# Value weights 48 instead of 32 columns into their tile, and dummy products in FFN block 0 in place of a shifted copy

## The chip, the cores and the metric

The kernel runs on one core of a Trainium2 chip. The core's engines work side by side: TensorE (PE in the profile) multiplies, VectorE (DVE), ScalarE (ACT) and GpSimd (POOL) do the elementwise work, and SyncE (SP) issues transfers. The metric is the device time of one execution in microseconds (us), as the median of several runs. Columns below are columns of 4 bytes in a tile of 128 partitions.

## The reference

The kernel computes two layers over 512 tokens of width 1024 in fp32. Each layer has a mixer and an FFN, each between norms that are modulated by a conditioning vector. Layer 0 mixes with a gated recurrence (HGRN2), layer 1 with dilated attention in three groups of windows. Cut to its core:

```python
for layer in range(DEPTH):                       # 2
    mod = (cond @ ada_w[layer] + ada_b[layer])[:, None, :]
    sh1, sc1, g1, sh2, sc2, g2 = jnp.split(mod, 6, axis=-1)
    u = rms_norm(h, norm_g[layer, 0]) * (1.0 + sc1) + sh1
    y = hgrn2_mixer(...) if layer % 2 == 0 else dilated_attention_mixer(...)
    h = h + (1.0 + g1) * rms_norm(y, norm_g[layer, 1])
    u = rms_norm(h, norm_g[layer, 2]) * (1.0 + sc2) + sh2
    y = swiglu_ffn(u, ffn_w_in[layer], ffn_w_out[layer])
    h = h + (1.0 + g2) * rms_norm(y, norm_g[layer, 3])

def swiglu_ffn(u, w_in, w_out):
    gate, up = jnp.split(u @ w_in, 2, axis=-1)
    return (jax.nn.silu(gate) * up) @ w_out

# dilated_attention_mixer, its first step (3 groups, 8 heads of 128)
proj = (u @ w_in).astype(jnp.float32).reshape(B, S, N_GROUPS, 3, ATT_HEADS, ATT_HEAD_DIM)
q, k, v = proj[:, :, gi, 0], proj[:, :, gi, 1], proj[:, :, gi, 2]   # q and k with rope
```

## The kernel before

**Products in three parts.** Every fp32 operand of a large product is cut into a high part, rounded to a shorter format (fp32r), and a low part, the rest. One product is then three of the engine's: high by high, high by low, low by high. ACT writes the high parts (`act.copy`), DVE the low ones (`dve.tensor_sub`). In a matmul of the kernel the first operand is stationary (128 columns, loaded before) and the second is moving (256 or 512 columns stream past it). `uh` and `ul` hold the two parts of the layer's activations, eight tiles of 128 features by 512 tokens each.

**Seven products for eight.** Large products are cut into two halves on both sides and done by a scheme with seven half products in place of eight (`seven_products` for the input weights of both FFNs). Its 256-wide products leave the 512 tokens as two halves.

**An FFN.** `ffn` does a part of the 22 feature tiles of the input product plainly (512-wide, L576 to L578) and gives the rest to `seven_products`: tiles 6 to 21 in layer 0, 4 to 21 in layer 1. So its loop `for i in range(len(fs))` has 16 blocks in layer 0 and 18 in layer 1. The text calls one pass of the loop a block, and i == 0 is block 0. A block has seven calls of `run`, in this order: (first, B11), (both, T3), (u2, t2), (first, B21), (u4, t1), (u2, T4), (u4, B22). A `run` issues 12 products of 256 columns (four of the contraction's tiles by three parts), all from L963. `R` is the pair of weight tiles with the halves as they are, `Sm` the pair with sums of halves. They are written one block ahead by ACT and DVE, with POOL for one of the sums. The order of all engines in the loop is written out by hand (`manual_schedule`).

**Places in a tile.** `R0` is the number of columns by which such weight tiles begin inside their allocation, so that the stationary operand of the 256-wide products begins 16 columns on. For the moving operand `B11`, block 0 reads the first 256 columns of `uh` and `ul` in place. In block 0, after the first halves of feature tiles 0 to 3 were read, `shift` copies them 144 columns on, into columns 144 to 399 of the same tiles, with four copies on ACT and four on DVE; blocks 1 and later read the copy. B21 and B22 are read in place, T3, T4, t1 and t2 from the tiles `th` and `tl`.

**Attention.** The projections of layer 1 are laid out by a planner, which places each piece of work by its cost and by when its data are due (`PE`, `ACT`, `DVE` with a cost in us; `products` for groups of matmuls, which come out at L1981). The values of groups 1 and 2 are done by `value_unit`, four units of 14 runs each with 12 products (seven half products, each in two column parts). Here the activations are stationary, and the weights, cut into 256 columns, are the moving operand. `split_place(V0)` gives each pair of weight tiles its place, `V0` columns in. Units 1 and 2 run from 741.75 us, 3 and 4 from 943.80 us, between scores (`scores_of`) and transposes. The products of queries and keys of these groups use the seven products too, with weights at `R0` as the stationary operand.

**The engines' queues.** Each engine takes its instructions in order. The loads of weights go through SP's queue and are issued when a raw buffer comes free.

Of the kernel before, what the change touches and what calls it, by code (L numbers as in the profile page):

```python
# [11 lines left out]
F32 = mybir.dt.float32  # L12
# [5 lines left out]
P = 128  # L18
# [15 lines left out]
MAGIC = 12582912.0  # L34
WHOLE = ("quarters", "half")

R0, V0 = 16, 32


class Stream:  # L40
# [100 lines left out]
class Plan:  # L141
# [95 lines left out]
    def run(self):  # L237

        ts = self.tasks
        for t in ts:  # L240
            for d in t["deps"]:
                ts[d]["outs"].append(t["id"])
        due = [0.0] * len(ts)
        for t in reversed(ts):
            at = min([due[o] - self.after(t, ts[o]) for o in t["outs"]], default=1e9)
            if t["goal"] is not None:
                at = min(at, t["goal"] + t["cost"])
            due[t["id"]] = at - t["cost"]
        tries = (self.trial(due, *rule) for rule in itertools.product((1, 2, 3, 5), (0.1, 0.2, 0.3), (5.0, 8.0, 1e9), (0.3, 1.0)))
        end, done, start = min(tries, key=lambda r: r[0])  # L250
        for t in done:
            t["start"], t["due"] = start[t["id"]], due[t["id"]]
        for t in done:
            if t["fn"]:
                t["fn"](t["eng"])
        return done
# [36 lines left out]
def block_kernel(tc, x, c, positions, ada_w, ada_b, norm_g, hgrn_w_in, lower, hgrn_norm_g, hgrn_w_out,  # L293
# [8 lines left out]
    with ExitStack() as ctx:  # L302
# [294 lines left out]
        class Turn:  # L597
# [61 lines left out]
            def u_of(self, t, q, ks=range(4)):  # L659
                if ks[0] == 0:  # L660
                    self.u[t, q] = fresh(self.pl, [P, 4, P], "u", 4)
                u, b = self.u[t, q], self.b[t][q]
                for k in ks:
                    kt = q * 4 + k
                    A, B, src = self.A[:, kt:kt + 1], self.B[:, kt:kt + 1], b[:, k * P:(k + 1) * P]
                    if q == 0:
                        act.activation(u[:, k], src, AF.Identity, bias=B, scale=A)
                    else:
                        dve.tensor_scalar(u[:, k], src, A, B, op0=OP.mult, op1=OP.add)
# [208 lines left out]
                    dve.tensor_sub(tl[:, k], t[k], th[:, k].bitcast(F32))  # L878
            return cut

        def seven_products(fs, mid, seeded, spare, th, tl):


            fs = list(fs)
            Q4 = lambda a: a.rearrange("p (s n) -> p s n", s=4)
            u_of = lambda r, c: [(uh[:, r * 4 + k, c * 256:c * 256 + 256], ul[:, r * 4 + k, c * 256:c * 256 + 256]) for k in range(4)]
            t_of = lambda i: [(th[:, i, k], tl[:, i, k]) for k in range(4)]
            B21, B22 = u_of(1, 0), u_of(1, 1)

            B11 = [u_of(0, 0), [(uh[:, k, 144:400], ul[:, k, 144:400]) for k in range(4)]]  # L890

            def shift():

                for a, b in ((112, 256), (0, 112)):
                    for copy, t in ((act.copy, uh), (dve.tensor_copy, ul)):
                        copy(t[:, 0:4, a + 144:b + 144], t[:, 0:4, a:b].bitcast(F32))
            t1, T3, T4, t2 = (t_of(i) for i in range(4))

            W = shared.rearrange("p a (b n) -> p (a b) n", b=2)
            H2 = lambda a: a.rearrange("p (a n) -> p a n", a=2)  # L900
            half = lambda b, k: b[:, k * 256:k * 256 + 256]
            ring = []
            raw = {}


            begun = [bank(t) for t in "abab"]

            class Sums:


                def __init__(self, i):
                    p = i % 2
                    self.first, self.both = (half(begun[2 * k + p], 0) for k in range(2))
                    self.u2, self.u4 = (half(seeded[2 * k + p], 0) for k in range(2))

            def places(i):

                p = i % 2
                if len(ring) <= p:
                    ring.append((spare if p == 0 else st.part_tiles(R0), st.part_tiles(R0)))  # L920
                return ring[p]

            def r_hi(i):
                if i < len(fs):
                    raw[i] = st.whole()
                    act.copy(places(i)[0][0][:, 0:1536], raw[i][:, 512:])

            def r_lo(i):
                hi, lo = places(i)[0]
                dve.tensor_sub(lo[:, 0:1536], raw[i][:, 512:], hi[:, 0:1536].bitcast(F32))  # L930

            def sum_a(i):
                r = Q4(raw[i])
                pool.tensor_add(r[:, 2], r[:, 2], r[:, 0])  # L934

            def sum_b(i):
                r = Q4(raw[i])
                dve.tensor_tensor(r[:, 0:2], r[:, 0:3:2], r[:, 1:2].broadcast_to((P, 2, 512)), op=OP.add)  # L938

            def sum_c(i):  # L940
                r = Q4(raw[i])
                dve.tensor_add(r[:, 3], r[:, 3], r[:, 1])

            def s_cut(i, k):
                src = Q4(raw[i])[:, 1:3] if k == 0 else Q4(raw[i])[:, 0:4:3]
                return [Q4(t)[:, 2 * k:2 * k + 2] for t in places(i)[1]] + [src]

            def s_hi(i, k):
                hi, lo, src = s_cut(i, k)
                act.copy(hi, src)  # L950

            def s_lo(i, k):
                hi, lo, src = s_cut(i, k)
                dve.tensor_sub(lo, src, hi.bitcast(F32))  # L954
                if k == 1:
                    raw.pop(i)
                    st.fill()

            def run(ps, w, o, us, begin):
                for kt in range(4):  # L960
                    a = slice(o + kt * P, o + (kt + 1) * P)
                    for m, (x, y) in enumerate(((0, 0), (0, 1), (1, 0))):
                        pe.matmul(ps, w[x][:, a], us[kt][y], start=begin and kt + m == 0, stop=kt == 3 and m == 2,  # L963
                                  skip_group_check=True)

            def gate_of(i, s):
                act.activation(W[:, 1], s.u4, AF.Silu)

            def value_of(i, s):
                dve.tensor_add(W[:, 3], W[:, 6 + i % 2], s.both)  # L970
                dve.tensor_add(W[:, 2], W[:, 4 + i % 2], s.u2)
                dve.scalar_tensor_tensor(H2(mid(fs[i])), W[:, 2:4], -1.0, W[:, 0:2], op0=OP.mult, op1=OP.mult)

            with tc.manual_schedule(engines=ORDERED):
                r_hi(0)
                r_lo(0)
                sum_a(0)
                sum_b(0)
                sum_c(0)
                for k in range(2):  # L980
                    s_hi(0, k)
                    s_lo(0, k)
                r_hi(1)
                before = None
                for i in range(len(fs)):
                    more = i + 1 < len(fs)
                    R, Sm = places(i)
                    s = Sums(i)
                    run(s.first, R, 0, B11[i > 0], True)
                    run(s.both, Sm, 1024, T3, True)  # L990
                    if before:
                        gate_of(i - 1, before)
                    act.copy(s.u2, s.first)
                    if more:
                        r_lo(i + 1)
                        sum_a(i + 1)
                    if before:
                        value_of(i - 1, before)
                    run(s.u2, Sm, 0, t2, False)
                    run(s.first, R, 1024, B21, False)  # L1000
                    act.copy(W[:, 4 + i % 2], s.both)
                    act.copy(s.u4, s.u2)
                    if i == 0:
                        shift()
                    run(s.u4, Sm, 512, t1, False)
                    run(s.u2, R, 512, T4, False)
                    if more:
                        sum_b(i + 1)
                        s_hi(i + 1, 0)
                        sum_c(i + 1)  # L1010
                        s_hi(i + 1, 1)
                        s_lo(i + 1, 0)
                        s_lo(i + 1, 1)
                    act.copy(W[:, 6 + i % 2], s.u4)
                    act.activation(W[:, 0], s.first, AF.Silu)
                    run(s.u4, Sm, 1536, B22, False)
                    if more:
                        r_hi(i + 2)
                    before = s
                gate_of(len(fs) - 1, before)  # L1020
                value_of(len(fs) - 1, before)

        def ffn(l, first, close, nxt, side):
            turns.close()
            close()
            with ExitStack() as fx:
# [4 lines left out]
                with ExitStack() as qx:  # L1031
# [6 lines left out]
                    for j in range(PLAIN[l]):  # L1038
# [14 lines left out]
                        if j == 0:  # L1053
                            cut()
                            fixed.close()
                    seven_products(range(2 * PLAIN[l], NF), mid, pss, spare, th, tl)
                fl.drain()
                roll = fx.enter_context(tc.tile_pool(name=f"roll{l}", bufs=1, side=bass.opposite_side(side)))
                y0 = [bank("mm") for _ in range(NT)]
# [1440 lines left out]
```

## Time and profile before

| what | value |
|---|---|
| median of 3 runs | 1509.28 us (1507.06 to 1509.78) |
| profiled execution, its own time | 1508.73 us |
| its span | 1507.0 us |
| mean granted TensorE clock | 0.993 |
| TensorE busy | 1477.4 us |
| DVE busy | 1096.8 us |
| ACT busy | 797.3 us |
| `seven_products`, layer 0, block 0 to the output product | 391.05 to 544.96 us |
| `seven_products`, layer 1, block 0's second product to the output product | 1207.90 to 1380.89 us |
| values of units 1 and 2 | 741.75 to 782.25 us |

A row of the timeline has the start, the duration, the engine, the line, the operation, the tile written and the tiles read, the shapes and a count, where neighbours of one form are drawn together. A matmul's duration reaches over its pipeline, so that neighbours overlap: the distance of two starts says how fast the engine goes on, the duration does not. In matmul rows `hiq` and `loq`, or `spare`, are the weights' parts, `uh`, `ul`, `th`, `tl` and `apart` those of the activations; the tile named first behind the arrow is the moving operand, the second the stationary one (`hiq,apart` has the value weights moving). A row of busy windows has the window, its length, the busy time with a count for each engine asked for, the granted clock, the DMA share and GB/s.

### The profile page before, as it was taken

What the parts mean: (1) busy time and instruction counts of PE and PEld (TensorE: products, weight loads), DVE (VectorE), ACT (ScalarE), POOL (GpSimd) and SP (SyncE); (2) the same over time, 40 slices, a digit from 0 to 9 for tenths busy, and PEclk for the clock granted to TensorE, in tenths of its full rate; (3) what the DMA queues carried; (4) which work ended last, traced back from release to release, by engine and by line L of the source; (5) the groups of instructions that cost most, each with busy time, mean ns of one, the idle gap of its engine ahead of it and who ended that gap; (6) DMA issues with size and microseconds to landing.
All of it is one profiled execution on the core that took longest, in us unless ns stands there. A gap on an engine that the chain in (4) does not pass through costs nothing. (4 is left out here: it accounts for less than half of the span.)

```text
span 1507.0 us, 25055 instructions
## 1 busy us (share of the span) xinstructions
PE 1477.4 (98%) x9807; PEld 1323.1 (88%) x9807; DVE 1096.8 (73%) x1816; ACT 797.3 (53%) x1474; POOL 197.5 (13%) x174
## 2 busy tenths in 40 slices
PE   8999998999999999999999999999999999999998
PEld 6777787888999997788999999999988899999886
DVE  4577677578688876777788877878766978887533
ACT  4433342464455542256637878567875655555231
POOL 1011013031111110222001010001012211110100
PEclk9999999999999999999999999999999999999999
DMA  9554553315333345634234443254343333434531
GB/s 307 179 173 138 184 168 112 112 57 157 93 107 108 107 155 206 226 136 140 82 121 137 131 129 94 81 161 123 91 154 126 97 100 113 113 111 142 199 110 56
DMA packets 210151, 201.09 MB, mean 133 GB/s; under 512 B 8248, under 2 KB 167920, under 8 KB 209776
## 3 DMA queue, kind: packets, MB, share of 16 engines
q1 hardware_dynamic: 207056, 192.71, 40.7%
q10 hardware_dynamic: 1952, 6.65, 1.2%
q8 instruction: 77, 1.26, 0.3%
q0 software_dynamic: 1024, 0.13, 0.2%
q14 instruction: 42, 0.34, 0.1%
HBM read 192.31 MB, written 5.31 MB: 131 GB/s over the span
## 5 line engine op out<-in xcount | busy, mean ns | idle before, releaser
L91 DVE TENSOR_TENSOR lo<-raw,hi 128x2048 fp32r<-128x2048 f32 x43 | 103.2, 2402 | 62.5 <-ACT hi L90 62.4
L90 ACT CAST hi<-raw 128x2048 fp32r<-128x2048 f32 x43 | 82.1, 1909 | 123.6 <-DMA raw<-in_ffn_w_out_dram 51.9
L576 PE MATMUL ps_mm<-uh,hi 128*128 128x512 f32 (+1 forms) x400 | 146.2, 366 | 0.0
L577 PE MATMUL ps_mm<-ul,hi 128*128 128x512 f32 (+1 forms) x400 | 144.8, 362 | 1.0 <-DVE ul L676 1.0
L578 PE MATMUL ps_mm<-uh,lo 128*128 128x512 f32 (+1 forms) x400 | 144.2, 360 | 0.0
L1981 PE MATMUL ps_mm<-apart,hiq 128*128 128x256 f32 (+1 forms) x608 | 142.0, 326 | 0.1
L1981 PEld LDWEIGHTS ps_mm<-apart,hiq 128*128 128x128 f32 x608 | 99.9, 189 | 8.3 <-ACT xs L2095 0.3
L1981 PE MATMUL ps_mm<-apart,loq 128*128 128x256 f32 (+1 forms) x304 | 97.4, 320 | 0.4 <-DVE loq L2117 0.4
L963 PE MATMUL ps_mm<-tl,hiq 128*128 128x256 f32 x340 | 93.9, 276 | 0.0
L963 PE MATMUL ps_mm<-th,loq 128*128 128x256 f32 x340 | 93.9, 276 | 0.0
L963 PE MATMUL ps_mm<-th,hiq 128*128 128x256 f32 x340 | 93.9, 276 | 0.0
L954 DVE TENSOR_TENSOR loq<-raw,hiq 128x1024 fp32r<-128x1024 f32 x68 | 80.3, 1222 | 18.6 <-ACT hiq L950 18.6
L576 PEld LDWEIGHTS ps_mm<-uh,hi 128*128 128x128 f32 x400 | 75.5, 189 | 18.4 <-issue 6.7
L577 PEld LDWEIGHTS ps_mm<-ul,hi 128*128 128x128 f32 x400 | 75.7, 189 | 12.5 <-DVE ul L676 1.4
L578 PEld LDWEIGHTS ps_mm<-uh,lo 128*128 128x128 f32 x400 | 75.5, 189 | 12.6 <-issue 1.1
L576 PE MATMUL ps_mm<-hi,oh 128*128 128x512 f32 x208 | 82.3, 396 | 4.2 <-ACT hi L90 4.2
L934 POOL TENSOR_TENSOR raw<-raw 128x512 f32<-128x512 f32 x34 | 44.8, 1316 | 304.6 <-DVE spare L930 138.6
L577 PE MATMUL ps_mm<-lo,oh 128*128 128x512 f32 x208 | 81.4, 392 | 0.0
L950 ACT CAST hiq<-raw 128x1024 fp32r<-128x1024 f32 x68 | 68.1, 1049 | 17.5 <-DVE raw L938 15.9
L1981 PE MATMUL ps_mm<-uh,hiq 128*128 128x256 f32 x256 | 71.8, 281 | 0.0
L1981 PE MATMUL ps_mm<-ul,hiq 128*128 128x256 f32 x256 | 71.2, 278 | 0.0
L1981 PE MATMUL ps_mm<-uh,loq 128*128 128x256 f32 x256 | 71.2, 278 | 0.0
(479 smaller groups left out, 4636.4 us busy)
## 6 DMA issues: line engine op xcount, KB each, us to landing
raw<-in_ada_w_dram SPq DMA_DIRECT2D x40, 1024.0 KB, 5.0
raw<-in_ffn_w_in_dram SPq DMA_DIRECT2D x136, 256.0 KB, 4.0
raw<-in_ffn_w_out_dram SPq DMA_DIRECT2D x22, 1024.0 KB, 4.8
raw<-in_attn_w_in_dram SPq DMA_DIRECT2D x64, 256.0 KB, 4.6
raw<-in_hgrn_w_in_dram SPq DMA_DIRECT2D x12, 1024.0 KB, 5.3
raw<-in_attn_w_in_dram SPq DMA_DIRECT2D x12, 1024.0 KB, 4.9
raw<-in_ffn_w_in_dram SPq DMA_DIRECT2D x10, 1024.0 KB, 5.0
raw<-in_attn_w_in_dram SPq DMA_DIRECT2D x16, 512.0 KB, 4.9
```

What stands on the lines that cost most here:

```text
L90: self.nc.scalar.copy(hi, t)
L91: self.nc.vector.tensor_sub(lo, t, hi.bitcast(F32))
L576: pe.matmul(ps, ah, bh, start=start, stop=False, skip_group_check=part)
L577: pe.matmul(ps, ah, bl, start=False, stop=False, skip_group_check=part)
L578: pe.matmul(ps, al, bh, start=False, stop=stop, skip_group_check=part)
L934: pool.tensor_add(r[:, 2], r[:, 2], r[:, 0])
L950: act.copy(hi, src)
L954: dve.tensor_sub(lo, src, hi.bitcast(F32))
L963: pe.matmul(ps, w[x][:, a], us[kt][y], start=begin and kt + m == 0, stop=kt == 3 and m == 2, skip_group_check=True)
L1981: pe.matmul(dst(), x, y, start=begin and i == 0, stop=i == len(todo) - 1, skip_group_check=True)
```

## The change

The value weights begin 48 columns in instead of 32. In `seven_products`, `B11` is always read in place; the shifted copy and the blocks' reading of it are gone. In block 0, after the first run, `aside` products with a moving operand 16 columns on, `uh[:, 0, 16:272]`, are issued into `s.both`; the next run begins that sum anew, so that their result is overwritten. `aside` is 1 in layer 0 and 3 in layer 1.

```diff
-R0, V0 = 16, 32
+R0, V0 = 16, 48
...
-        def seven_products(fs, mid, seeded, spare, th, tl):
+        def seven_products(fs, mid, seeded, spare, th, tl, aside):
...
-            B11 = [u_of(0, 0), [(uh[:, k, 144:400], ul[:, k, 144:400]) for k in range(4)]]
-
-            def shift():
-
-                for a, b in ((112, 256), (0, 112)):
-                    for copy, t in ((act.copy, uh), (dve.tensor_copy, ul)):
-                        copy(t[:, 0:4, a + 144:b + 144], t[:, 0:4, a:b].bitcast(F32))
+            B11 = u_of(0, 0)
...
-                    run(s.first, R, 0, B11[i > 0], True)
+                    run(s.first, R, 0, B11, True)
+                    if i == 0:
+                        for _ in range(aside):
+                            pe.matmul(s.both, R[0][:, 0:P], uh[:, 0, 16:272], start=True, stop=True, skip_group_check=True)
                     run(s.both, Sm, 1024, T3, True)
...
-                    if i == 0:
-                        shift()
...
-                    seven_products(range(2 * PLAIN[l], NF), mid, pss, spare, th, tl)
+                    seven_products(range(2 * PLAIN[l], NF), mid, pss, spare, th, tl, (1, 3)[l])
```

## The prediction

> **What bounds the kernel now.** I read the page first: the sums by engine, the slices with the clock, and the chain of work that ended last.
>
> ```profile
> span 1507.0 us, 25055 instructions
> PE 1477.4 (98%) x9807; PEld 1323.1 (88%) x9807; DVE 1096.8 (73%) x1816; ACT 797.3 (53%) x1474; POOL 197.5 (13%) x174
> PEclk9999999999999999999999999999999999999999
> PE 21%; issue 1%; ACT 0%; DVE 0%; POOL 0%; DVEq 0%; POOLq 0%; ACTq 0%
> ```
>
> TensorE is busy for 98% of the span at an even clock, and the chain, as far back as it could be followed, has next to nothing but its products. Where it is so full, a saving on another engine is worth nothing in itself, and the time changes by the number of products and by the distance from one product's start to the next one's. The durations on the page are no help with that distance, because their ends are modelled and overlap. So I went to the timeline and to busy windows cut exactly at starts, in FFN block 0 of layer 0 and the block after it.
>
> ```profile
> 391.05:400.94 9.89, 9.89 (x84) 1.00 0.01 2
> 400.94:544.96 144.02, 144.02 (x1262) 1.00 0.40 118
> 410.56:420.16 9.60, 9.60 (x87) 1.00 0.38 109
> ```
>
> A block has 7 runs of 12 products, 84 in all (in windows that begin in the middle of the work the count holds a few that were still draining). Block 0 takes 9.89 us, 117.7 ns a product. Block 2, with the same products and the same clock, takes 9.60. Its starts show where the difference lies:
>
> ```profile
> 410.56 0.28 PE L963 MATMUL ps_a<-uh,spare 128*128 128x256 f32 x1
> ...
> 411.98 0.29 PE L963 MATMUL ps_a<-th,hiq 128*128 128x256 f32 x1
> ...
> 413.36 0.28 PE L963 MATMUL ps_mm<-th,hiq 128*128 128x256 f32 x1
> ```
>
> Its first run, the one that reads the shifted copy (144 columns on, that is 16 beyond a multiple of 128), takes 1.42 us, the second 1.38, and the other five, from 413.36 to 420.16, take 6.80: 1.36 a run, 113.3 ns a product. So one instruction form at one clock has three paces here: **113.3** (fast), **117.7** (block 0, slow) and about 119 to 120 (shifted run). A pace, once taken, stays through many runs. Block 0 never becomes fast; the first shifted run comes after it and the pace is fast from then on:
>
> ```profile
> 400.94 0.28 PE L963 MATMUL ps_b<-uh,hiq 128*128 128x256 f32 x1
> 401.07 0.28 PE L963 MATMUL ps_b<-ul,hiq 128*128 128x256 f32 x1
> ...
> 402.38 0.29 PE L963 MATMUL ps_b<-th,hiq 128*128 128x256 f32 x1
> 402.51 0.28 PE L963 MATMUL ps_b<-tl,hiq 128*128 128x256 f32 x1
> 402.63 0.28 PE L963 MATMUL ps_b<-th,loq 128*128 128x256 f32 x1
> 402.74 0.28 PE L963 MATMUL ps_b<-th,hiq 128*128 128x256 f32 x1
> ```
>
> Two products after the last shifted one the distance is 0.11. My reading: the shifted run is what moves the stream out of the slow pace, and every later block pays for the shift again without needing it.
>
> **The FFN blocks, layer 0.** Without the shift, blocks 1 to 15 cost 15 × 84 × 113.33 ns = 142.80 us if they stay fast, against 144.02 in the second window above: **−1.22**. In block 0 the dummy stands behind the first run. The 72 products after it took 72 × 117.7 = 8.48 us and take 72 × 113.33 = 8.16 if they become fast: −0.32. The dummy adds one product, 0.12 by the first interval from 400.94, and the stream needs two slower intervals before it is fast, 0.01: +0.13. Layer 0: **−1.41**.
>
> **Layer 1** has 18 blocks and three dummies.
>
> ```profile
> 1207.90:1217.68 9.78, 9.78 (x84) 1.00 0.02 5
> 1217.68:1380.89 163.21, 163.21 (x1430) 1.00 0.40 117
> 1218.03 0.28 PE L963 MATMUL ps_b<-uh,hiq 128*128 128x256 f32 x1
> ...
> 1219.11 0.29 PE L963 MATMUL ps_b<-th,hiq 128*128 128x256 f32 x1
> ```
>
> Blocks 1 to 17: 17 × 84 × 113.33 = 161.84 against 163.21, **−1.37**. Block 0: −0.32 again; three dummies at 0.118 are +0.35 and the way out costs some 0.02. Layer 1: **−1.32**. Do one and three suffice? In layer 0 the shifted run's first interval is already the long one (0.13 from 400.94 to 401.07), and the stream's slow pace repeats with every three products, so that the dummy, 72 products earlier, meets the stream as that first product did. In layer 1 the shifted run comes to its steady 0.12 from its fourth product on (1218.03 to 1219.11 is 1.08 for nine), and what follows steady 0.12 becomes fast at the start of every later block, as at 411.98 above. So the counts fit what each block shows. That does not prove that one product does what twelve did; the bounds if it does not are these: a block that stays slow takes 9.89, so layer 0 would cost 15 × 9.89 = 148.35 against 144.02, **+4.33**, and 0.12 for the dummy; layer 1 17 × 9.89 = 168.13 against 163.21, **+4.92**, and 0.35.
>
> The eight **removed copies** (four on ACT, four on DVE, once in each layer) and the ACT and DVE work of a block lie beside the products:
>
> ```profile
> 411.00:421.00 10.00, 10.00 (x90) 10.00 (x89) 8.22 (x9) 5.76 (x10) 1.29 (x1) 1.00 0.38 111
> ```
>
> The columns are TensorE, its weight loads, DVE, ACT and POOL. DVE has 1.8 us to spare in ten and ACT 4.2, so the copies' end is worth nothing, and a block shortened by 0.08 doesn't reach that slack. The dummy reads weights that the first run already read and writes a bank half that the next run begins anew; it adds no wait. What follows layer 0's blocks has one wait:
>
> ```profile
> PE ps_mm L576 <- ACT hi L90: 4.2, 1, 4.2
> 601.80 1.90 ACT L90 CAST hi<-raw 128x2048 fp32r<-128x2048 f32 x1 [7.26 <-DMA raw<-in_ffn_w_out_dram]
> ```
>
> The weights for the output product arrive late there. If that load goes out earlier by what the blocks gain, the wait stays 4.2 and the 1.41 arrives; if it starts no earlier, the wait grows and 1.41 is lost. The load is one of a series whose buffers come free behind the blocks' work, so I let it pass; none of it is the other end.
>
> **The values.** The 256-wide weight tile is the moving operand, 32 columns in before and 48 after. Two stretches use it:
>
> ```profile
> 742.05:782.25 40.20, 40.20 (x336) 1.00 0.34 109
> 948.11:986.43 38.32, 38.32 (x324) 1.00 0.43 125
> ```
>
> 335 distances of 120.0 ns, and 323 of 118.6. What sets the pace seems to be the distance of the stationary operand's start from the moving one's. It is +16 columns in the unshifted FFN products and in those of queries and keys (weights 16 in, moving tile at a multiple of 128), and these are fast or slow; it is 16 − 144 = −128 in the shifted run, about 120; and 0 − 32 = −32 in the values, 118.6 to 120.0. After the change the values have −48. Counted around 64 columns, −128 is 0, −32 is 32, and −48 is +16, the place of the fast and slow paces. The 64 is my reading; with a longer round −48 would be a new place, and its end is the worst case below. Products of queries and keys, at +16, show how each pace is entered:
>
> ```profile
> 816.74 0.59 PE L1981 MATMUL ps_mm<-apart,hiq 128*128 128x256 f32 x2
> 817.17 0.28 PE L1981 MATMUL ps_mm<-apart,loq 128*128 128x256 f32 x1
> ...
> 817.87 0.28 PE L1981 MATMUL ps_mm<-apart,loq 128*128 128x256 f32 x1
> ...
> 887.49 0.48 PE L1981 MATMUL ps_mm<-apart,hiq 128*128 128x256 f32 x2
> 887.81 0.28 PE L1981 MATMUL ps_mm<-apart,loq 128*128 128x256 f32 x1
> ...
> 888.87 0.28 PE L1981 MATMUL ps_mm<-apart,loq 128*128 128x256 f32 x1
> ```
>
> The first, behind 256-wide scores, is at 0.70 for six products and then fast, 0.34 for three; the second, behind 128-wide ones, runs 1.06 for nine, slow. The first stretch of the values is entered behind 256-wide scores, as at 816.74, the second behind 128-wide ones. Fast, the stretches gain 335 × 6.67 = **2.23** and 323 × 5.3 = **1.71**; slow, 335 × 2.3 = 0.77 and 323 × 0.9 = 0.29. The worst end is that nothing changes in the first and the second goes to 120.0: 323 × 1.4 = +0.45. I take fast for both, the first more surely than the second. But in the first stretch another engine is nearly as full:
>
> ```profile
> 742.00:752.00 10.00, 10.00 (x85) 10.00 (x84) 10.00 (x16) 6.27 (x7) 0.00 (x0) 1.00 0.13 36
> ...
> 762.00:772.00 10.00, 10.00 (x86) 10.00 (x85) 9.93 (x10) 4.68 (x5) 0.00 (x0) 1.00 0.01 2
> ...
> 950.00:960.00 10.00, 10.00 (x87) 10.00 (x86) 8.54 (x18) 5.92 (x14) 0.76 (x1) 1.00 0.68 191
> PE ps_mm L1981 <- DVE loq L2117: 0.4, 1, 0.4
> ```
>
> DVE, which cuts the low parts of the weights, is busy for 10.00 and 9.93 of two stretches of 10 us, and the products wait for such a cut once already, soon after. A part of the 2.23 will turn into a wait; between none and all I take 1.5 as arriving. In the second stretch DVE has 1.5 us free in ten, and 1.71 passes.
>
> **Sum.** −1.41 − 1.32 − 1.5 − 1.71 = −5.94 on the profiled execution's 1508.73: 1502.8. That execution is 0.55 below the median of the runs shown, 1509.28, which gives **1503.3** as a median.
>
> By the Trainium skill ("TensorE: Matmul & The Clock Gate", "Back-to-back issue gap") the distance of two products is the moving columns at 2.4 GHz and 2.5 ns more, 109.2 ns for 256, and the place of an operand has no part in it. This trace disagrees, with 113.3, 117.7 and 120.0 for one form at an even clock; going by the page, the values would gain nothing and the dummies would only cost.
>
> **The rivals.**
> - *The values go slow, or fast in one stretch only, and the FFN blocks as forecast.* For it: the entry behind 128-wide scores at 887.49 ended slow. Slow in both: −2.73 − 0.77 − 0.29 = −3.8, 1505.5; slow in the first and fast in the second −5.2, 1504.1. Against it: 816.74 and that 118.6 at 948 is already another pattern than 120.0.
> - *The dummies don't turn the stream*, the case on the other side. It is decided at the first products of the second run of block 0: if these are still 117.7 apart, nothing later turns them, since the shifted runs are gone, and the whole layer stays slow. Both layers: 4.33 + 0.12 + 4.92 + 0.35 = +9.7, less 3.2 from the values: +6.5, **1515.8**. One layer alone: +4.45 − 1.32 − 3.2 = −0.1 or +5.27 − 1.41 − 3.2 = +0.7, about 1509.6. For it: twelve products did it before, not one; and a block that loses the fast pace in 144 us has nothing that brings it back. Against it: the five fast runs of every block hold.
> - *Waits swallow it*: the DVE cuts hold the values (1.5 lost) and the wait at 601.80 takes 1.41: −3.0, 1506.2; with slow values in the second stretch as well −1.32 − 0.29 = −1.6, 1507.7.
> - *The place of the operand isn't the cause*, the shifted copy being slow as a copy: then the dummies alone remain, 4 × 0.12 = +0.5, less 1.22 and 1.37 from the copies' end; 1507.2. Against it: the values are at 120.0 with no copy. [...]
>
> **How the numbers follow.** Forecast 0.43; values weaker 0.25; both layers slow 0.11; one layer slow 0.08; waits 0.09; not the place 0.04. About 0.2%, 3.0 us, can be told from no change, so faster means below 1506.3. That holds for the forecast, for 0.22 of the weaker values and some of the waits: 0.68. Slower means above 1512.3: both layers and some of one, 0.13, raised to 0.15 for what a broken pace may do further on. Same: 0.17. The range from 1501.8 (all of the 2.23 arrives, and some of the products behind the values turn fast) to 1510.8 holds all but both layers slow and a little below. The forecast's own range is 1502.0 to 1504.8.
>
> **What would show it.** The first run of block 1 should be 1.36 us, and blocks 1 to 15 and 1 to 17 142.8 and 161.8. Block 0 should be at 113.3 from a few products behind the dummies on; 117.7 there is the rival. The two stretches of the values should show 113.3 ns; where 117.7 stands, the entry decided it. A new wait for the low cuts between 742 and 793, or a wait above 4.2 for the output weights, would show a gain given back. Any pace other than these three in the values would break my reading of what sets it.

## The result, and the profile after

| | before | changed |
|---|---|---|
| median, first measurement (8 runs each) | 1509.62 us | 1504.97 us |
| ratio to before, 95% interval | | 0.9969 (0.9958 to 0.9980) |
| median, second measurement (32 and 12 runs) | 1511.22 us | 1508.81 us |
| ratio to before, 95% interval | | 0.9979 (0.9966 to 0.9993) |

The changed kernel is faster, by 0.2 to 0.3%. The page of the changed kernel, its span and sums by engine:

```profile
span 1502.8 us, 25057 instructions
PE 1473.6 (98%) x9811; PEld 1320.4 (88%) x9811; DVE 1095.2 (73%) x1812; ACT 793.5 (53%) x1470; POOL 197.5 (13%) x174
```

TensorE has four instructions more and is busy 3.8 us less: the same work at a closer distance, as the bound of before asks for. The busy windows of the FFN products, cut at the starts of block 0, of block 1 and of the output product in layer 0, then of block 0's second run, of block 1 and of the output product in layer 1:

```profile
390.23:399.95 9.72, 9.72 (x84) 1.00 0.02 5
399.95:542.75 142.80, 142.80 (x1262) 1.00 0.40 119
1206.62:1214.80 8.18, 8.18 (x73) 1.00 0.03 8
1214.80:1376.63 161.83, 161.83 (x1430) 1.00 0.40 118
```

Blocks 1 to 15 take 142.80 us and blocks 1 to 17 161.83, which is 113.3 ns a product. The timeline behind the dummies (L986), layer 0 first:

```profile
391.64 0.28 PE L986 MATMUL ps_a<-uh,spare 128*128 128x256 f32 x1
391.76 0.28 PE L957 MATMUL ps_a<-th,hiq 128*128 128x256 f32 x1
...
392.36 0.28 PE L957 MATMUL ps_a<-th,loq 128*128 128x256 f32 x1
392.47 0.28 PE L957 MATMUL ps_a<-th,hiq 128*128 128x256 f32 x1
392.58 0.28 PE L957 MATMUL ps_a<-tl,hiq 128*128 128x256 f32 x1
...
1206.26 0.52 PE L986 MATMUL ps_a<-uh,spare 128*128 128x256 f32 x3
1206.62 0.29 PE L957 MATMUL ps_a<-th,hiq 128*128 128x256 f32 x1
...
1207.09 0.28 PE L957 MATMUL ps_a<-tl,hiq 128*128 128x256 f32 x1
1207.20 0.28 PE L957 MATMUL ps_a<-th,loq 128*128 128x256 f32 x1
```

One dummy costs 0.12, the three 0.36. In layer 0 the distance falls to 0.11 behind the sixth product, in layer 1 behind the third (1206.86), and it stays so for the layer. The two stretches of the values:

```profile
739.35:778.81 39.46, 39.46 (x336) 1.00 0.34 111
944.52:982.57 38.05, 38.05 (x325) 1.00 0.40 123
```

335 distances in 39.46 us are 117.8 ns, and 323 in 38.05 are 117.8 as well: the slow pace, in both. By stages, the change is worth 391.05 to 544.96 against 390.23 to 542.75, 1.39 us, in layer 0; 1.38 in blocks 1 to 17 of layer 1, less 0.05 in its block 0 (9.83 us from its second product on, against 9.78); 0.74 and 0.27 in the values: 3.7 us. The rest of the difference between the two profiles is the start-up, which the change doesn't touch (block 0 of layer 0 begins at 391.05 and 390.23), and small waits of both signs further on.

### The profile page after: what moved, and what is told of

Its sections match the earlier page's. It is cut to its first block, busy times and chain, and to the rows that moved or that the text cites. A ratio compares the mean times of both kernels' runs of the same rounds, so it can differ in the third digit from the quotient of the medians.

```text
span 1502.8 us, 25057 instructions
## 1 busy us (share of the span) xinstructions
PE 1473.6 (98%) x9811; PEld 1320.4 (88%) x9811; DVE 1095.2 (73%) x1812; ACT 793.5 (53%) x1470; POOL 197.5 (13%) x174
```

## The experiments

**Each part by itself.** The FFN part with the value weights at 32 columns, and the values' part with the old FFN code:

```diff
-R0, V0 = 16, 48
+R0, V0 = 16, 32
```

> Value weights at 32 columns again, the FFN part as changed. Theory (the two parts add): blocks 1 to 15 of layer 0 take 142.8 us and blocks 1 to 17 of layer 1 161.8, the values 120.0 and 118.6 ns a product as before; the time is 2.7 us below before's (ratio 0.9982). Rival (the gain of one layer is given back in a wait behind it): the blocks show the same figures, the time is only 1.3 us below (0.9991).

> Value weights at 48 columns, FFN as before. Theory (the later attention gives the values' gain back: the changed kernel's trace is 3.75 us ahead at the end of the second value stretch and only 2.66 ahead at the FFN of layer 1): both stretches at 117.8 ns a product, 0.74 and 0.27 us less, and the time within 0.3 us of before's (ratio 0.9998 to 1.0002). Rival (what is lost there is chance of that execution or comes from the FFN part): the time is 1.0 us below (0.9993).

The FFN part alone gave a ratio of 1.0000 (0.9991 to 1.0009), the values alone 1.0016 (1.0006 to 1.0026). Neither was as expected, and the two don't add up to 0.9969. Their profiles have the stage gains all the same: blocks 1 to 15 and 1 to 17 take 142.80 and 161.84 in the FFN part's, the first stretch of the values 39.46 in the other. The start of block 0 in the FFN part's profile, and in that of the values' part:

```profile
393.74 0.28 PE L957 MATMUL ps_a<-uh,spare 128*128 128x256 f32 x1
```

```profile
388.31 0.28 PE L963 MATMUL ps_a<-uh,spare 128*128 128x256 f32 x1
```

Up to this point the two kernels and before's issue the same instructions, and the three profiles stand at 393.74, 388.31 and 391.05: the start-up of single executions is 5.4 us apart. In the profile of the values' part there is besides, near the end of the attention, a wait of TensorE that before's has not in this length (there it is 0.71). From its timeline and its busy windows:

```profile
1123.36 2.53 PE L2320 MATMUL ps_a<-ident,h 128*128 128x128 f32 x8 [3.56 <-ACT h L2305]
```

```profile
1123.30:1126.30 3.00, 2.94 (x10) 0.50 0.00 0
1126.30:1129.30 3.00, 3.00 (x12) 0.52 0.00 0
```

TensorE waits 3.56 us for the last head's scaled probabilities, and then runs at a granted clock of 0.50 for some 6 us. The same place in the changed kernel's profile:

```profile
1120.75 1.96 PE L2315 MATMUL ps_a<-ident,h 128*128 128x128 f32 x8 [0.99 <-ACT h L2300]
```

```profile
1120.70:1123.70 3.00, 2.73 (x13) 1.00 0.00 0
```

0.99 us and the full clock. The long wait and the half clock together cost the profile of the values' part 5.0 us between 1100 and 1150, by the starts of like instructions, more than either part is worth. Whether this belongs to a kernel or to chance was the question of the second measurement.

**No dummy, and dummies at the usual relation.** Layer 0 has none here, layer 1 three that read their operand in place:

```diff
-                            pe.matmul(s.both, R[0][:, 0:P], uh[:, 0, 16:272], start=True, stop=True, skip_group_check=True)
+                            pe.matmul(s.both, R[0][:, 0:P], uh[:, 0, 0:256], start=True, stop=True, skip_group_check=True)
...
-                    seven_products(range(2 * PLAIN[l], NF), mid, pss, spare, th, tl, (1, 3)[l])
+                    seven_products(range(2 * PLAIN[l], NF), mid, pss, spare, th, tl, (0, 3)[l])
```

> The changed kernel without a dummy in layer 0, and in layer 1 three dummies that read their moving operand in place (relation +16 columns, as every other product of the block) in place of 16 columns on. Theory (it is the products at the other relation that turn the stream): both layers stay at 117.8 ns, blocks 1 to 15 of layer 0 take 148.4 us and blocks 1 to 17 of layer 1 168.1; the time is 12 us above the changed kernel's, about 1517. Rival (any three products more turn it): layer 1 stays at 161.8, the time is about 6 above. Other rival (no product is needed, the change of run order alone does it): layer 0 at 142.8.

Busy windows of blocks 1 and later, layer 0 and layer 1:

```profile
400.62:549.01 148.39, 148.39 (x1262) 1.00 0.38 114
1224.89:1393.08 168.19, 168.19 (x1430) 1.00 0.38 113
```

Both layers stay slow from end to end, at the figures that the theory named; the time of the one run was 1520.92, with a long wait in the late attention (3.23) in it. So the shifted run did turn the stream in the old code, its removal alone costs, and three extra products of the usual kind don't replace it. The same three with the operand 16 columns further on do, in the changed kernel: what turns the stream is the operand's place.

**The numbers exchanged**, three dummies in layer 0 and one in layer 1:

```diff
-(1, 3)[l]
+(3, 1)[l]
```

> Three dummies in layer 0 and one in layer 1, the changed kernel otherwise. Theory (a few products at the other relation turn the stream wherever it stands): both layers fast, 142.8 and 161.8 us as in the changed kernel, the time the same within noise. Rival (the number must fit the place at which the stream stands, so that one or both fail): a layer that fails takes 148.4 or 168.1 us, 5.5 to 6.5 us more.

```profile
400.57:543.37 142.80, 142.80 (x1262) 1.00 0.40 119
1209.03:1217.51 8.48, 8.48 (x74) 1.00 0.04 12
1217.51:1385.70 168.19, 168.19 (x1430) 1.00 0.38 113
```

Three turn layer 0 as one does. One doesn't turn layer 1: its second to seventh runs take 8.48 us and all blocks after them stay slow, 168.19. The rival holds for layer 1, where the price was 6.4 us in that layer and the run's time 1513.54. The number has to fit the place.

**Other places for the value weights**, 112 and 16 columns:

```diff
-R0, V0 = 16, 48
+R0, V0 = 16, 112
```

> The changed kernel with the value weights at 112 columns in place of 48: relation -112, which is +16 when counted around 64 columns, as -48 is. Theory (the round is 64): the first stretch of the values shows 117.8 or 113.3 ns a product and no other pace. Rival (the round is longer, and 48 is good by itself): another pace, 118.6 to 120 ns, 40.2 us instead of 39.5 for the first stretch.

> The changed kernel with the value weights at 16 columns: relation -16, which is 48 around 64, a place that nothing in the kernel used so far. Theory A (0 and 32 are the slow places and every odd multiple of 16 is good): 117.8 or 113.3 ns. Rival B (only +16 is good): 118.6 to 120 ns a product.

The first stretch of the values, with 112 and with 16 columns:

```profile
740.22:779.68 39.46, 39.46 (x337) 1.00 0.34 111
```

```profile
741.39:780.85 39.46, 39.46 (x337) 1.00 0.36 111
```

39.46 us in both, as with 48. The relation −16 gives the same pace, so +16 isn't the only good place. A round of 64 columns fits 48 and 112, but it isn't shown: all relations seen at 113.3 or 117.8 (16, −16, −48, −112) are odd multiples of 16, and the two at 118 to 120 (−32, −128) are multiples of 32. A round of 32 columns would say as much, and no run tells the two apart.

**Dummies for the values.** Before the third run of a unit (the second product, `m4`), dummies whose moving operand begins 16 columns further on, a relation of −64:

```diff
+                def first():
+                    for _ in range(dummies):
+                        pe.matmul(b.t[:, 0:256], us(0, 0)[0], p.t[0][:, o * 1024 + 16:o * 1024 + 272], start=True, stop=True, skip_group_check=True)
...
-                ps["m4"] = run("a", 0, 1, w_of(2))
+                ps["m4"] = run("a", 0, 1, w_of(2), 3 if hf == 0 else 0)
```

> The changed kernel with three dummies more, moving operand 16 columns further on (relation -64, counted 0), before the third run of the first unit of each of the two stretches of values. Theory (such products turn a slow stream anywhere): some products behind them the values are at 113.3 ns to the stretch's end, 312 x 4.45 ns - 0.36 = 1.0 us less in the first stretch and about as much in the second. Rival (the number must fit the place): the stretch stays at 117.8, 0.36 us more.

> As vd3 with one dummy in place of three. Theory (any number turns it): 1.27 us less in each stretch than in the changed kernel. Rival (the number must fit the place, as one failed in the FFN of layer 1): 117.8 ns stays in at least one stretch, 0.12 us more there.

The condition on `hf` put them before both units of the first stretch and none of the second. The first stretch with three, from the end of the first turned run to the second set of dummies; and the whole first stretch with one:

```profile
747.29:764.96 17.67, 17.67 (x158) 1.00 0.38 128
```

```profile
737.91:777.60 39.69, 39.69 (x337) 1.00 0.34 110
```

With three, the 13 runs up to the second unit's dummies take 17.67, which is 1.36 a run: fast. The whole stretch takes 38.81, so that it is fast behind the second set too; the second stretch, which has none in this run, stays at 117.8. With one, twice, the stretch takes 39.69, the changed kernel's 39.46 and two dummies: not turned. The single times, 1507.57 and 1502.78, go the other way round, because of the start-up and the late wait; they decide nothing.

**The second measurement**, all on one chip with 32 runs of before, and a kernel with three dummies in each stretch:

```diff
-                ps["m4"] = run("a", 0, 1, w_of(2))
+                ps["m4"] = run("a", 0, 1, w_of(2), 3 if i == 0 else 0)
```

> The changed kernel once more, beside the two that follow on the same chip. By the stages' sums of its first profile (FFN 1.38 and 1.32, values 0.74 and 0.28) the time is 3.7 us below before's, ratio 0.9975; what lies beyond that either way is chance of the start-up and of the gather behind the last head's statistics, or something that the sums lack.

> The FFN part alone once more (its first runs showed 1.0000 where 0.9982 was expected, though its profile had both layers' gain in full). Theory (the first runs happened to have slower start-ups, 2.7 us by that profile, and more of the long waits in the late attention): the time is 2.7 us below before's, 0.9982. Rival (this kernel has the slower start-up or the long wait in most of its executions): 1.0000 again.

> The values' part alone once more (its first runs showed 1.0016, its profile a wait of 3.6 us and half the clock behind it, together 5.0 us, near 1123 us). Theory (chance): 1.0 us below before's, 0.9993. Rival (this kernel's transfers meet at that place in most of its executions): 1.0016 again, half of the runs or more at 1512 us and over.

> The changed kernel with three dummies before the third run of the first unit in each stretch of the values (in vd3 they stood in the first stretch twice and in the second not at all). Theory: the first stretch is 0.74 + 1.39 - 0.37 = 1.75 us shorter than before's, the second 0.28 + 1.0 = 1.3 if three fit there too; the time is 2.0 us below the changed kernel's on the same chip. Rivals: three don't fit the second stretch, which then is 0.36 longer than the changed kernel's and stays at 117.8; or a DVE wait behind the first stretch takes its gain.

| kernel | first ratio | second ratio |
|---|---|---|
| changed | 0.9969 (0.9958 to 0.9980) | 0.9979 (0.9966 to 0.9993) |
| FFN part alone | 1.0000 (0.9991 to 1.0009) | 0.9975 (0.9963 to 0.9987) |
| values' part alone | 1.0016 (1.0006 to 1.0026) | 1.0001 (0.9990 to 1.0013) |
| changed, values turned too | | 0.9964 (0.9951 to 0.9977) |

The first ratios of the two parts are from another chip than the second ones. The FFN part moved from 1.0000 to 0.9975, further than its first interval allows: two measurements of one kernel differ by more than the part's 2.7 us are worth (0.0018). On the second chip the FFN part alone did as well as both parts together, and the values' part showed no gain in either measurement, though its stages gain 1.0 us in the profile: in the whole time that 1.0 us isn't shown. The changed kernel's second profile shows one thing that differs between executions. The late attention in it, from the timelines of DVE, GpSimd and TensorE:

```profile
1116.02 0.77 POOL L2283 DMA_DIRECT2D so<-scr  x1 [3.68 <-DMA scr<-so]
1122.16 0.17 DVE L2292 TENSOR_TENSOR wM<-so 128x8 f32<-128x8 f32 x1 [6.11 <-DMA so<-scr]
1124.52 2.52 PE L2315 MATMUL ps_a<-ident,h 128*128 128x128 f32 x8 [4.21 <-ACT h L2300]
```

and in its first:

```profile
1114.64 0.76 POOL L2283 DMA_DIRECT2D so<-scr  x1 [2.86 <-DMA scr<-so]
1118.39 0.17 DVE L2292 TENSOR_TENSOR wM<-so 128x8 f32<-128x8 f32 x1 [2.88 <-DMA so<-scr]
```

One and the same kernel: a 4 KB gather is followed by its reader 3.75 us after its issue in one execution and 6.14 in the other, and TensorE waits 0.99 or 4.21. (The store ahead of the gather took longer too, 3.68 against 2.86.) So the long wait isn't fixed to a kernel. It stood in four of the fourteen profiles (the values alone, the one without dummies, the one with 16 columns and this one).

Two loads of 1 MB for the output weights go out at this place, and the gather's delay goes with its place behind them. In the four profiles it was issued 2.3 to 2.8 us behind the first load and reached its reader after 5.5 to 6.1; in the other ten it was issued 1.8 to 2.2 us behind and took 3.6 to 4.7. No run moved the loads, so that they delay it is argued and not shown.

Nor is it shown that the long wait comes by chance alone. All four profiles have the value weights moved, and none of the three with 32 columns has it. The runs' mean granted clocks differ by kernel on the first chip (6.8 us at one half lower the mean over 1507 us by 0.002): 0.992 or less in 1 of 23 runs of before, 4 of 11 of the FFN part and 7 of 12 of the values' part. On the second chip it was 8 of 32, 2 of 12 and 4 of 12. Whether the changed timing brings the wait more often stays open.

The kernel with both stretches turned, in busy windows: the first stretch whole, its part from the third turned run on, and the same of the second; then two windows with DVE in third place:

```profile
741.85:780.30 38.45, 38.26 (x337) 1.00 0.35 113
747.65:780.30 32.65, 32.65 (x291) 1.00 0.41 134
946.04:983.08 37.04, 36.84 (x324) 1.00 0.42 119
950.44:983.08 32.64, 32.64 (x290) 1.00 0.48 135
```

```profile
742.00:752.00 10.00, 10.00 (x90) 10.00 (x89) 10.00 (x14) 6.07 (x7) 0.00 (x0) 1.00 0.13 34
762.00:772.00 10.00, 10.00 (x90) 10.00 (x90) 9.93 (x11) 4.69 (x5) 0.00 (x0) 1.00 0.04 11
```

24 runs in 32.65 and in 32.64 are 1.36 a run: fast in both. Against the changed kernel, 39.46 − 38.45 = 1.01 and 38.05 − 37.04 = 1.01 us are gained with the dummies paid, 2.0 as expected. Its median, 1504.95, is the lowest of the four on that chip; its interval overlaps the changed kernel's, so that the times alone don't prove the step, but the windows do. And DVE is as full as it was, 10.00 and 9.93, while TensorE has no wait in the stretch.

## Why the prediction was right, and where it wasn't

**The time** fell, as forecast, but the sum was too large: the stages gained 3.7 us where 5.9 stood. That the first measurement came as near as 4.7 us is in part luck; the second had 2.4.

**The FFN blocks** came out by the sum: 142.80 and 161.83 against 142.80 and 161.84, block 0 of layer 0 9.72 against 9.70 (the way out took six products where two were counted), the dummies 0.12 and 0.36 against 0.12 and 0.35. Its reading of the mechanism holds: the run without dummies stays slow in both layers, and three with the operand in place don't help. The argument for "one and three suffice" was weaker than the sum: three would have done for both, one for layer 0 alone, as the exchanged numbers show. The rival on the other side had its deciding point right: where the second run of block 0 stayed at 0.118, the whole layer did.

**The values** are the step that failed: "I take fast for both, the first more surely than the second." Both came out slow, 0.74 and 0.27 us where 2.23 and 1.71 stood (or 1.5, as counted). The rival with slow values in both had 0.77 and 0.29 and 1505.5; the first measurement had 1504.97. The new relation did bring the products to the pair of paces 113.3 and 117.8. What was wrong was to read the entries at 816.74 and 887.49 as a rule: fast behind 256-wide scores, slow behind 128-wide ones. The entry at 739.05 follows 256-wide scores too, and was slow in every profile with the weights at 48. The rule fails the other way as well. One run of the values stands by itself ahead of the second stretch, behind 128-wide transposes, and in the changed kernel it is fast without any dummy:

```profile
940.59 0.39 PE L1976 MATMUL ps_mm<-hiq,apart 128*128 128x256 f32 x2
...
941.16 0.28 PE L1976 MATMUL ps_mm<-loq,apart 128*128 128x256 f32 x1
```

Five distances take 0.57 here, and the ten from 940.47 to 941.61 take 1.14, 114 ns. It is 114 or 115 in all ten profiles with 48 or 112 columns, and 118 in the three with 32. What went before doesn't name the pace by itself; what decides it stays open.

**The cut for DVE** in the first stretch was wrong too: with 113.3 ns in 24 of its 28 runs the stretch gets no wait. A second engine at 10.00 of 10 us is no proof that it sets the pace: here TensorE went faster and never waited for it.

**The rest.** No run took out the copies alone, but there is nothing that they could have given: the blocks' 142.80 us are 1260 distances of 113.33, with no idle time of TensorE. The wait for the output weights behind layer 0 did grow in the changed kernel's profile:

```profile
PE ps_mm L576 <- ACT hi L90: 4.9, 1, 4.9
```

0.7 us more, which the text on record calls a gain given back. But the products behind it then come sooner: at the starts of like products near 618 us the profile is 2.4 us ahead of before's, 0.8 of it the start-up and 1.39 the blocks. In the ten profiles that have layer 0's gain, the stretch from the end of the blocks to these products is between 0.8 us shorter and 1.0 us longer than in before's, and 0.2 longer on average, so that most of the gain passes. The prediction had no term for chance in single profiles: the start-up, and the late wait with the half clock, move one execution by up to 5 us each, more than the whole change.

The Trainium skill ("TensorE: Matmul & The Clock Gate", "Back-to-back issue gap") gives the gap of an isolated product by its columns alone, which comes to an estimate of 109.2 ns for 256, with no term for the operands' places. The runs with 32, 48, 112 and 16 columns disagree, with 120.0 in the first stretch for the first and 117.8 for the other three, and 113.3 with 48 once turned.

## What to carry to other kernels

Where one engine is full, measure the distance between starts and not the durations, and look for two distances of one instruction form: the difference times the count is what can be had. If a form can hold two paces, a few odd products at the right place may turn the slow one into the fast, but their number has to be tried at each place. And when a change is worth 0.2%, compare the windows of the stages that it touches: two measurements of the same kernel's ratio differed by 0.25% here.

## What the runs showed of the hardware

- 256-wide fp32r products with the same clock hold 113.3 or 117.8 ns for as long as the stream isn't broken, 24 runs and more, when the stationary operand begins 16 or −48 columns from the moving one (with −16 and −112 such a stretch was seen at 117.8); they take 118 to 120.0 with −32, and 118 to 120 with −128. Why these places differ, and why one dummy (relation 16 − 16 = 0) doesn't turn the stream in layer 1 where three do, stays open.
- A wait of 3.2 to 4.2 us came with a granted clock of one half in all four profiles that had it, for 3.4 us in two of them and 6.8 in the others. By the Trainium skill ("TensorE: Matmul & The Clock Gate", "What's actually happening") an idle window of about 3.4 us does that. The four agree only in part: in the waits of 3.23 and 3.56 us the clock fell 2.0 and 2.5 us after the wait began. The second profile of the values' part disagrees, with a shorter wait. Its timeline and the window behind it:

```profile
1122.68 2.10 PE L2320 MATMUL ps_a<-ident,h 128*128 128x128 f32 x8 [1.00 <-ACT h L2305]
```

```profile
1124.00:1127.00 3.00, 3.00 (x11) 0.56 0.00 0
```

A wait of 1.00 us and a clock of 0.56 behind it, where the kernel with three dummies in the values' first stretch had waited 2.09 there and kept 1.00. Why stays open.
